# Expert stage of a two-block model: how each pair of experts gets its token rows, four more weight tiles, and the place of the overflow loop

## The chip, the cores and the metric

The kernel runs on one core of one Trainium2 chip. Its time is the device time in microseconds (us). Before the change it is 2866.49 us, the median of 3 runs (2866.16 to 2867.72). The engines are PE (TensorE, matmuls), DVE (VectorE), ACT (ScalarE), POOL (GpSimd) and SP (SyncE, which here only issues DMAs). The engines run side by side and meet at semaphores.

## The reference

Two transformer-like blocks run one after the other on 512 tokens of width 1024. The change touches only the last part of the second block, a mixture of experts (`hier_moe`), and the final norm behind it:

```python
ht = h.reshape(T, D)                                   # T = 512 tokens, D = 1024
grp = jnp.argmax(g_logits, axis=-1)                    # one of 4 groups
top_p, top_i = lax.top_k(e_prob, TOP_K)                # 2 of the group's 8 experts
expert = grp[:, None] * EXP_PER_GROUP + top_i          # 2 of 32 experts per token
...
xb = ht[tok]                                           # rows of the tokens of one expert
hid = jax.nn.silu(xb @ w_gate[e]) * (xb @ w_up[e])     # 1024 -> 512
return hid @ w_down[e]                                 # 512 -> 1024
...
y = jnp.zeros((T, D), f32).at[buf_tok].add(y_blocks * buf_w[:, None])
x = x + y ; return rmsnorm(x, final_norm_g)
```

Each expert has three float32 matrices of 2 MiB, so 32 experts read 192 MiB.

## The kernel before, in words

**Pairs of experts.** The stage `Moe.run` works on 16 pairs. Each expert has 64 slots for tokens, so a pair fills 128 slots: the first expert is in rows 0 to 63 and the second in rows 64 to 127. `route` works out for each of a token's two choices its slot, 64 * expert + rank. Tokens beyond an expert's 64 slots are done by `overflow`, a loop whose count `nov` is read at run time (`For_i`, L1860). With these inputs the loop's body doesn't run: no matmul of its shapes is in the trace.

**Gathering tokens by matmul.** `rows` turns the 8 tiles of the residual into token rows and splits each into a high and a low half (`h2`, in 16 tiles `x` of the pool `px`). `gather` (L1726) builds 0/1 matrices by comparing slot numbers with a row 0, 1, 2, ... (`iota`): `A` in bf16, one for each choice, and `oh`, their sum. Every second pair, 64 matmuls (L1748) multiply `h2` by `oh` and give the tokens of two pairs, 256 columns, which ACT scales into `X`. `gs` multiplies `A` by three bf16 pieces of the gate weight and of the norm's factor.

**The work of a pair.** `up` multiplies by the gate matrices (32 matmuls on the trace, L1772), then by the up matrices (32 more, L1772). `down` transposes the result (4, L1815), lets `turned` transpose `oh` (4, L1801) into `oT`, and multiplies by the down matrices (32, L1824). `combine` (16 matmuls, L1842, and 8 additions on DVE, L1850) adds the result of the pair before into the tokens; it is woven into the next pair by `add`, so that no engine waits for it.

**Weights.** `load_w` issues 12 DMAs of 1 MiB for a pair from SP, in the order gate, up, down. They go into 13 tiles `we`, which exist while the stage before still runs, and 4 tiles `we2`: 17 in turn. A load waits until the tile that it overwrites has been read by its last matmul, and all loads wait in one queue in order.

**Order.** PE's order in the pairs is as written (`manual_schedule`); a scheduler places the other engines' instructions. Pairs 0 to 13 run first, then their last `combine`, then the loop `overflow`, then pairs 14 and 15. At the loop all engines meet, and SP goes into it only when its loads have landed; `load(14, AH)` therefore puts few loads of the next pair ahead of it.

Of the kernel before, what the change touches and what calls it, by code (L numbers as in the profile page):

```python
# [115 lines left out]
class Ker:  # L116
    def __init__(self, ctx, tc, I):
        self.tc, self.nc, self.I = tc, tc.nc, I
        self.scopes = []
        self.base = ctx.enter_context(tc.tile_pool(name="base", bufs=1))  # L120
        self.px = ctx.enter_context(tc.tile_pool(name="px", bufs=16))
# [7 lines left out]
        nc.sync.dma_start(self.ident, I["c_ident"])  # L129

# [1328 lines left out]
def consts3():  # L1459
# [4 lines left out]
    c["c_iota"] = np.ascontiguousarray(np.broadcast_to(np.arange(256, dtype=f), (128, 256)))  # L1464
# [19 lines left out]
SBM = dict(we2=4, X=1, oh=4, A=8, hid=1, hT=1, y=4, oT=1, rel=2, gs=2)  # L1484
AH = 3
# [3 lines left out]
class Moe:  # L1489
    CAP = 64  # L1490

    def __init__(self, K, V):
# [7 lines left out]
        self.iota = cst("iota", (128, 256), I["c_iota"])  # L1500
# [62 lines left out]
    def load_piece(self, e):  # L1563

        def get(q, i, k, d=0):
            w, n = self.weights()[i]
            t = self.K.px.tile([128, 512], F32, name="rstd", tag="rstd", bufs=1)
# [5 lines left out]
    def rows(self, x3):  # L1573

        K, nc = self.K, self.nc
        self.h2 = [[None] * 2 for _ in range(4)]
        b = K.t("X", (128, 4, 512))
        at = [K.t("hid"), K.t("oT"), K.t("hT")] + [b[:, j, :] for j in range(4)]
        for h in range(2):
            for t in range(4):  # L1580
# [3 lines left out]
                hi, lo = K.xt(), K.xt()  # L1584
                if not at:
                    K.split(ps, hi, lo)
                else:
                    x = at.pop()
                    nc.scalar.copy(hi, ps)
                    nc.scalar.copy(x, ps)  # L1590
                    nc.gpsimd.tensor_sub(lo, x, hi.bitcast(F32))
                self.h2[t][h] = (hi, lo)
# [26 lines left out]
    def route(self):  # L1619
# [60 lines left out]
        self.gr = one("grs", (128, 3, 2, 4, 2), BF16)  # L1680
# [4 lines left out]
        for i in range(3):  # L1685
            nc.vector.tensor_copy(self.gr[:, i], gr)
            if i < 2:
                nc.vector.tensor_sub(gr, gr, self.gr[:, i])
# [37 lines left out]
    def gather(self, rel, n, follow=lambda X, k: None):  # L1726
# [3 lines left out]
        oh, A = [], []  # L1730
        for t in range(4):
            A.append([K.t("A", (128, n), BF16) for _ in range(2)])
            nc.vector.tensor_scalar(A[t][1], self.iota[:, 0:n], rel[:, 1, t:t + 1], None, op0=ALU.is_equal)  # L1733
            o = K.t("oh", (128, n), F32R)
            nc.vector.scalar_tensor_tensor(o, self.iota[:, 0:n], rel[:, 0, t:t + 1], A[t][1], op0=ALU.is_equal,  # L1735
                                           op1=ALU.add)
            oh.append(o)
        for t in range(4):
            nc.gpsimd.tensor_scalar(A[t][0], self.iota[:, 0:n], rel[:, 0, t:t + 1], None, op0=ALU.is_equal)
        X = K.t("X", (128, 8, n))  # L1740
        w = 512 // n
        for k0 in range(0, 8, w):
            ps = K.p("x", (128, w, n))
            for k in range(k0, k0 + w):
                c = slice((k % 4) * 128, (k % 4 + 1) * 128)
                for t in range(4):
                    for j in range(2):
                        nc.tensor.matmul(ps[:, k - k0, :], self.h2[t][k // 4][j][:, c], oh[t], start=(t == 0 and j == 0),  # L1748
                                         stop=(t == 3 and j == 1))
            for k in range(k0, k0 + w):  # L1750
                nc.scalar.activation(X[:, k, :], ps[:, k - k0, :], AF.Copy, scale=self.g[:, k:k + 1])
            for k in range(max(k0 - w, 0), k0):
                follow(X, k)
        for k in range(8 - w, 8):
            follow(X, k)

        def gs(p):
            m = min(n, 128)
            ps = K.p("x", (128, 3, 2))
            for i in range(8):  # L1760
                t, a = divmod(i, 2)
                nc.tensor.matmul(ps[0:m], A[t][a][:, p * 128:p * 128 + m], self.gr[:, :, a, t, :], start=(i == 0), stop=(i == 7))
            s = K.t("gs", (128, 4))
            nc.vector.tensor_reduce(s[0:m, 0:2], ps[0:m].rearrange("p j c -> p c j"), axis=AX.X, op=ALU.add)
            nc.vector.tensor_scalar(s[0:m, 2:3], s[0:m, 1:2], 0.5, None, op0=ALU.mult)
            nc.vector.tensor_mul(s[0:m, 3:4], s[0:m, 1:2], s[0:m, 2:3])
            return s
        return X, oh, gs
# [5 lines left out]
    def up(self, X, w, n_ex, gs, pg=None, then=lambda hid: None, between=lambda: None):  # L1774
# [4 lines left out]
        if pg is None:  # L1779
            pg = K.p("g")  # L1780
            for k in range(8):
                self.proj(pg, X, w, n_ex, 0, k)
        gs = gs()
        hid = K.t("hid")
        nc.scalar.activation(hid[n], pg[n], AF.Tanh, scale=gs[n, 2:3])
# [6 lines left out]
        nc.vector.scalar_tensor_tensor(hid[n], hid[n], gs[n, 3:4], pu[n], op0=ALU.mult, op1=ALU.mult)  # L1792
        return hid, gs

    def turned(self, n_ex, oh):

        K, nc = self.K, self.nc
        np_ = 64 * n_ex
        ps = K.p("y")
        for t in range(4):  # L1800
            nc.tensor.transpose(ps[0:np_, t * 128:(t + 1) * 128], oh[t].bitcast(F32), K.ident)  # L1801
        o = K.t("oT", dt=F32R)
        if np_ < 128:
            nc.gpsimd.memset(o[np_:128].bitcast(F32), 0.0)
        nc.vector.tensor_copy(o[0:np_], ps[0:np_])
        return o

    def down(self, w, n_ex, hid, gs, between):
# [9 lines left out]
        o = between()  # L1818
# [13 lines left out]
        return o, ys  # L1832

    def combine(self, o, ys, ts=range(4), first=False, done=None):

        K, nc = self.K, self.nc
        for t in ts:
            s = slice(t * 128, (t + 1) * 128)
            for d in range(2):
# [3 lines left out]
                if first:  # L1843
                    hi, lo = self.h2[t][d]
                    a = self.acc[t][d] = K.t("h")
                    nc.vector.tensor_add(a, ps, hi.bitcast(F32))
                    nc.vector.tensor_add(a, a, lo.bitcast(F32))
                else:
                    a = self.acc[t][d]
                    nc.vector.tensor_add(a, a, ps)  # L1850
# [3 lines left out]
    def overflow(self):  # L1854
# [5 lines left out]
        with tc.For_i(0, n, 1) as i:  # L1860
# [4 lines left out]
            X, oh, gs = self.gather(rel, 64)  # L1865
            w = self.load_piece(e)
            hid, g = self.up(X, w, 1, lambda: gs(0))
            self.combine(*self.down(w, 1, hid, g, lambda: self.turned(1, oh)))

    def run(self, ctx, x3, out):  # L1870
        K, nc, I = self.K, self.nc, self.K.I
        K.scope(ctx, "mo", SBM, PSM)
        self.acc = [[None] * 2 for _ in range(4)]
# [3 lines left out]
        next(steps)  # L1877
# [29 lines left out]
        def add(*ts):  # L1907
            if late:
                o, ys, first = late
                self.combine(o, ys, ts, first)  # L1910

        def pair(i):
            nonlocal X, oh, gs, late
            q, p = divmod(i, 2)
            load(i)
            pg = None
            if i == 0:
                pg = K.p("g")
# [90 lines left out]
```

## Time and profile before

| | |
|---|---|
| time of the profiled execution | 2866.79 us |
| its span | 2865.0 us |
| median of the runs shown | 2866.49 us |
| PE busy | 2787.5 us, 97% of the span |
| DVE, ACT, POOL busy | 1721.1 us, 1070.5 us, 179.0 us |
| mean TensorE clock granted | 0.986 |
| read from HBM | 415.91 MB |

All times below are us from the span's start, unless they are ns. The expert stage begins at about 2334 (the token rows) and ends with the span. PE is nearly always busy in every stage, so the share alone doesn't tell what a change is worth; what counts in the expert stage is how closely PE and the weight loads follow one another. [...]

### The profile page before, as it was taken

What the parts mean: (1) busy time and instruction counts of PE and PEld (TensorE: products, weight loads), DVE (VectorE), ACT (ScalarE), POOL (GpSimd) and SP (SyncE); (2) the same over time, 40 slices, a digit from 0 to 9 for tenths busy, and PEclk for the clock granted to TensorE, in tenths of its full rate; (3) what the DMA queues carried; (4) which work ended last, traced back from release to release, by engine and by line L of the source; (5) the groups of instructions that cost most, each with busy time, mean ns of one, the idle gap of its engine ahead of it and who ended that gap; (6) DMA issues with size and microseconds to landing.
All of it is one profiled execution on the core that took longest, in us unless ns stands there. A gap on an engine that the chain in (4) does not pass through costs nothing. (4 is left out here: it accounts for less than half of the span.)

```text
span 2865.0 us, 41006 instructions
## 1 busy us (share of the span) xinstructions
PE 2787.5 (97%) x15978; PEld 2027.6 (71%) x15978; DVE 1721.1 (60%) x3122; ACT 1070.5 (37%) x1992; POOL 179.0 (6%) x221
## 2 busy tenths in 40 slices
PE   8989999999999999998999999999999889999998
PEld 6779878888889888886776777777778664444543
DVE  6666666645566666648777778678775343333333
ACT  4355443333244433345544455445444231111112
POOL 3100000000000000013000000000013120000000
PEclk8999999999999999999999999999999989999999
DMA  5324222223234122234422233223238719999966
GB/s 171 96 67 146 75 82 95 96 96 105 95 112 146 59 96 95 94 114 142 139 75 84 87 90 103 82 78 98 65 110 322 269 64 400 417 415 420 419 269 265
DMA packets 176005, 447.70 MB, mean 156 GB/s; under 512 B 80928, under 2 KB 82144, under 8 KB 151232
## 3 DMA queue, kind: packets, MB, share of 16 engines
q1 hardware_dynamic: 175504, 444.16, 43.6%
q8 instruction: 127, 2.08, 0.3%
q0 software_dynamic: 304, 0.89, 0.1%
q14 instruction: 70, 0.57, 0.1%
HBM read 415.91 MB, written 29.08 MB: 155 GB/s over the span
## 5 line engine op out<-in xcount | busy, mean ns | idle before, releaser
L171 ACT CAST w<-wr 128x512 fp32r<-128x512 f32 x662 | 407.3, 620 | 758.5 <-PE ps_d L217 659.2
L216 PE MATMUL ps_d<-x,w 128*128 128x512 f32 x1624 | 659.8, 406 | 0.7 <-ACT w L171 0.7
L218 PE MATMUL ps_d<-x,w 128*128 128x512 f32 x1624 | 653.8, 403 | 4.1 <-DVE w L172 4.1
L217 PE MATMUL ps_d<-x,w 128*128 128x512 f32 x1624 | 654.3, 403 | 0.0
L172 DVE TENSOR_TENSOR w<-wr,w 128x512 fp32r<-128x512 f32 x662 | 471.3, 715 | 266.3 <-ACT w L171 261.6
L218 PEld LDWEIGHTS ps_d<-x,w 128*128 128x128 f32 x1624 | 306.1, 188 | 76.8 <-DVE w L172 4.7
L216 PEld LDWEIGHTS ps_d<-x,w 128*128 128x128 f32 x1624 | 306.5, 189 | 74.1 <-issue 4.3
L217 PEld LDWEIGHTS ps_d<-x,w 128*128 128x128 f32 x1624 | 306.6, 189 | 69.9 <-issue 2.9
L1772 PE MATMUL ps_g<-we,X 128*64 128x512 f32 x1024 | 226.8, 595 | 0.0
L216 PE MATMUL ps_d<-s,w 128*128 128x512 f32 x512 | 202.8, 396 | 0.0
L217 PE MATMUL ps_d<-s,w 128*128 128x512 f32 x512 | 202.6, 396 | 0.0
L218 PE MATMUL ps_d<-s,w 128*128 128x512 f32 x512 | 202.6, 396 | 0.0
L1772 PEld LDWEIGHTS ps_g<-we,X 128*64 128x64 f32 x1024 | 71.1, 137 | 137.8 <-issue 136.5
L1824 PE MATMUL ps_y<-we,hT 128*64 128x512 f32 x512 | 113.6, 595 | 0.5 <-ACT hT L1817 0.5
L217 PEld LDWEIGHTS ps_d<-s,w 128*128 128x128 f32 x512 | 96.1, 188 | 23.4 <-DVE s L172 0.6
L216 PEld LDWEIGHTS ps_d<-s,w 128*128 128x128 f32 x512 | 96.1, 188 | 22.8
L218 PEld LDWEIGHTS ps_d<-s,w 128*128 128x128 f32 x512 | 96.1, 188 | 22.7
L216 PE MATMUL ps_a<-x,w 128*128 128x512 f32 x232 | 92.1, 405 | 8.4 <-DVE gt L1428 5.2
L217 PE MATMUL ps_a<-x,w 128*128 128x512 f32 x232 | 93.3, 403 | 0.1
L218 PE MATMUL ps_a<-x,w 128*128 128x512 f32 x232 | 92.2, 399 | 0.0
L1824 PEld LDWEIGHTS ps_y<-we,hT 128*64 128x64 f32 x512 | 35.1, 137 | 67.7 <-issue 64.4
L1850 DVE TENSOR_TENSOR h<-h,ps_x 128x512 f32<-128x512 f32 x120 | 76.7, 681 | 7.4 <-PE ps_x L1842 6.4
(574 smaller groups left out, 4146.9 us busy)
## 6 DMA issues: line engine op xcount, KB each, us to landing
we<-in_w_exp_gate SPq DMA_DIRECT2D x64, 1024.0 KB, 12.0
we<-in_w_exp_up SPq DMA_DIRECT2D x64, 1024.0 KB, 12.1
we<-in_w_exp_down SPq DMA_DIRECT2D x64, 1024.0 KB, 12.6
wr<-in_w_in SPq DMA_DIRECT2D x83, 512.0 KB, 3.6
wr<-in_ffn_w_up SPq DMA_DIRECT2D x64, 512.0 KB, 3.2
wr<-in_ffn_w_down SPq DMA_DIRECT2D x32, 512.0 KB, 3.2
wr<-in_w_in_c SPq DMA_DIRECT2D x24, 512.0 KB, 3.2
wr<-in_w_in_ab SPq DMA_DIRECT2D x16, 512.0 KB, 4.2
```

The lines of the kernel that those rows point to most:

```text
L171: nc.scalar.copy(hi, x)
L172: nc.vector.tensor_sub(lo, x, hi.bitcast(F32))
L216: nc.tensor.matmul(ps, whi, xhi, start=start, stop=False)
L217: nc.tensor.matmul(ps, whi, xlo, start=False, stop=False)
L218: nc.tensor.matmul(ps, wlo, xhi, start=False, stop=stop)
L1772: self.nc.tensor.matmul(ps[e * 64:e * 64 + 64, :], X[:, k, e * 64:e * 64 + 64], w(e, i, k), start=(k == 0), stop=(k == 7))
L1824: nc.tensor.matmul(py[e * 64:e * 64 + 64, :], hT[:, f, e * 64:e * 64 + 64], w(e, 2, f, d), start=(f == 0), stop=(f == 3))
L1850: nc.vector.tensor_add(a, a, ps)
```

## The change

- `rows` copies the token rows whole (no split) into the accumulators `acc` and writes them to a DRAM buffer `hr` (8 DMAs of 256 KB, on SP). `combine` thereby loses its special first case.
- `index` replaces the 0/1 matrix `oh`. For one pair at a time it builds `A` with 128 columns (4 comparisons on POOL, 4 on DVE), multiplies it by token numbers (`tok`, 8 small matmuls), and turns the sum into a row number. Then come the 8 small matmuls by `gr`, as before.
- `gather` is now one indirect DMA on POOL's queue: 128 rows of 4 KB out of `hr` into `G` (512 KB). `columns` transposes `G` (8 transposes) and scales into `X` (2 multiplications on DVE).
- This runs a pair ahead (`ahead`): the comparisons of pair i+1 are placed at the start of pair i, the small matmuls between its gate and up matmuls, the transposes before its down matmuls.
- `back` gets `oT` by one comparison on DVE; the transposes of `turned` go.
- `we2` grows from 4 to 8 tiles (21 in all). The pool `px` (17 tiles of 2 KB) is placed on the other side of the memory and ends with the stage before.
- The loop `overflow` stands behind pair 0, with 8 of pair 2's loads ahead of it.

```diff
-SBM = dict(we2=4, X=1, oh=4, A=8, hid=1, hT=1, y=4, oT=1, rel=2, gs=2)
-AH = 3
+SBM = dict(we2=8, X=1, G=1, Xo=1, Go=1, A=8, hid=1, hT=1, y=4, oT=1, rel=2, gs=3, ix=2)
...
     def rows(self, x3):
...
-                self.h2[t][h] = (hi, lo)
+                a = self.acc[t][h] = K.t("h")
+                nc.scalar.copy(a, ps)
+                nc.sync.dma_start(self.hr[t * 128:(t + 1) * 128, h * 512:(h + 1) * 512], a)
...
-    def gather(self, rel, n, follow=lambda X, k: None):
+    def index(self, rel, n=128):
...
         for t in range(4):
...
+            A.append([K.t("A", (128, 128), BF16)[:, 0:n] for _ in range(2)])
+            for a, eng in enumerate((nc.gpsimd, nc.vector)):
+                eng.tensor_scalar(A[t][a], self.iota[:, 0:n], rel[:, a, t:t + 1], None, op0=ALU.is_equal)
+        yield
+        s, ix = K.t("gs", (128, 5)), K.t("ix", (128, 2))
+        def product(shape, of):
+            ps = K.p("x", shape)
             for i in range(8):
                 t, a = divmod(i, 2)
...
+                nc.tensor.matmul(ps[0:n], A[t][a], of(a, t), start=(i == 0), stop=(i == 7))
+            return ps[0:n]
+        nc.vector.tensor_reduce(s[0:n, 2:3], product((128, 2), lambda a, t: self.tok[:, t]), axis=AX.X, op=ALU.add)
+        nc.vector.tensor_scalar(ix[0:n, 0:1], s[0:n, 2:3], -1.0, 0.0, op0=ALU.add, op1=ALU.max)
+        self.token = ix.bitcast(I32)[:, 1:2]
+        nc.vector.tensor_copy(self.token[0:n], ix[0:n, 0:1])
+        yield
+        ps = product((128, 3, 2), lambda a, t: self.gr[:, a, t])
...
+    def gather(self, n=128, tag="G"):
+
+        G = self.K.t(tag, (128, 1024))
+        self.nc.gpsimd.indirect_dma_start(out=G[0:n], out_offset=None, in_=self.hr[:],
+                                          in_offset=bass.IndirectOffsetOnAxis(ap=self.token[0:n], axis=0))
+        return G
+
+    def columns(self, G, n=128, tag="X"):
...
+            for k in range(4):
+                nc.tensor.transpose(ps[:, k, :], G[0:n, (k0 + k) * 128:(k0 + k + 1) * 128], K.ident[0:n, 0:n])
+            nc.vector.tensor_mul(X[:, k0:k0 + 4, :], ps, self.g[:, k0:k0 + 4, None].to_broadcast([128, 4, n]))
+        return X
...
+    def back(self, n, s):
...
+        nc.vector.tensor_scalar(o[0:n], self.iota[0:n], 1.0, s[0:n, 2:3], op0=ALU.add, op1=ALU.is_equal)
...
+        def ahead(i):
...
+            part = self.index(rel)
+            next(part)
+            yield
+            next(part)
+            G = self.gather()
+            yield
+            yield next(part), G
...
+            def mid():
+                nonlocal coming
+                if i < 15:
+                    next(nxt)
+                    coming = next(nxt)
+                add(0)
+            hid = self.up(X, w, 2, gs, then, mid)
...
             def rest():
                 add(2, 3)
-                return self.turned(2, [x[:, s] for x in oh])
-            late = *self.down(w, 2, hid, g, rest), i == 0
...
+                if i < 15:
+                    columns.append(self.columns(coming[1]))
+            ys = self.down(w, 2, hid, gs, rest)
+            late = self.back(128, gs), ys
...
         with K.tc.manual_schedule(engines=PE):
-            for i in range(14):
-                pair(i)
+            load(0)
+            load(1)
+            pair(0)
             add(0, 1, 2, 3)
         late = None
-        load(14, AH)
+        load(2, 8)
         self.overflow()
         with K.tc.manual_schedule(engines=PE):
-            for i in (14, 15):
+            for i in range(1, 16):
                 pair(i)
-            self.combine(*late[:2], done=finish)
-
+            self.combine(*late, done=finish)
```

PE, one pair in the middle of the stage, before. `y`, `oT` belong to the combine of the pair before, `hid` is transposed for the down matmuls, `oh` and `x` are the 0/1 matrix and the split token rows.

```order
L1842 MATMUL ps_x<-y,oT 128x512 x4
L1772 MATMUL ps_g<-we,X 64x512 x16
L1842 MATMUL ps_x<-y,oT 128x512 x4
L1815 MATMUL ps_y<-ident,hid 128x128 x4
L1842 MATMUL ps_x<-y,oT 128x512 x8
L1801 MATMUL ps_y<-ident,oh 128x128 x4
L1824 MATMUL ps_y<-we,hT 64x512 x16
L1748 MATMUL ps_x<-oh,x 128x256 x64
```

PE at the same place, now. The row by `grs` is the last of the 8 small matmuls, behind the 8 by `tokb`.

```order
L1745 MATMUL ps_x<-grs,A 128x6
L1842 MATMUL ps_x<-y,oT 128x512 x4
L1787 MATMUL ps_g<-we,X 64x512 x16
L1842 MATMUL ps_x<-y,oT 128x512 x4
L1815 MATMUL ps_y<-ident,hid 128x128 x4
L1842 MATMUL ps_x<-y,oT 128x512 x8
L1772 MATMUL ps_x<-ident,G 128x128 x8
L1824 MATMUL ps_y<-we,hT 64x512 x16
L1787 MATMUL ps_g<-we,X 64x512 x16
```

The 64 matmuls of every second pair are gone and the 4 transposes of `oh` have become 8 of `G`, which wait for the indirect DMA.

SP from the last weight loads before the stage to the loop, now (before, the loads of the first 14 pairs stand there without a break).

```order
L1568 DMA we_21363<-in_w_exp_gate 128x2048
L1595 DMA hr<-h 128x512 x8
L1568 DMA we_21365<-in_w_exp_gate 128x2048
L1568 DMA we_21367<-in_w_exp_up 128x2048
...
L1568 DMA we<-in_w_exp_down 128x2048 x3
L1568 DMA we<-in_w_exp_gate 128x2048 x4
L1568 DMA we<-in_w_exp_up 128x2048 x4
L1853 TENSOR_LOAD nov
```

The 8 writes of token rows stand ahead of the last 6 of the 21 first loads; 11 more loads stand ahead of the loop's count, all others behind it.

POOL from the head of the stage to the pairs behind the loop, now (before, it has there 24 comparisons for `A` in a row).

```order
L1738 TENSOR_SCALAR A<-iota,rel 128x128 x8
L1761 DMA G<-hr,ix 128x1024 x2
L1853 TENSOR_LOAD nov
...
L1738 TENSOR_SCALAR A<-iota,rel 128x128 x6
L1761 DMA G<-hr,ix 128x1024
L1738 TENSOR_SCALAR A<-iota,rel 128x128 x4
```

The first gather stands behind the comparisons of pairs 0 and 1, and each later gather behind two comparisons of the pair after it.

## Rows read from the trace of the kernel before

**Rows 1.** The page: span in 40 slices, busy tenths of PE and DMA.
```profile
PE   8989999999999999998999999999999889999998
DMA  5324222223234122234422233223238719999966
```
**Rows 2.** Timeline of PE, pairs 2 and 3: start, us, engine, line, what.
```profile
2421.32 7.09 PE L1772 MATMUL ps_g<-we,X 128*64 128x512 f32 x32
2428.34 0.36 PE L1762 MATMUL ps_x<-grs,A 128*128 128x6 bf16 x8
...
2440.14 0.60 PE L1801 MATMUL ps_y<-ident,oh 128*128 128x128 f32 x4
2440.67 7.09 PE L1824 MATMUL ps_y<-we,hT 128*64 128x512 f32 x32
...
2447.58 7.04 PE L1772 MATMUL ps_g<-we,X 128*64 128x512 f32 x32
...
2473.89 7.84 PE L1748 MATMUL ps_x<-oh,x 128*128 128x256 f32 x64
2481.66 7.09 PE L1772 MATMUL ps_g<-we,X 128*64 128x512 f32 x32
```
**Rows 3.** Windows: stretch, us, five engines' busy us, PE clock, DMA share, GB/s.
```profile
2352.00:2358.00 6.00, 6.00 (x32) 5.29 (x34) 0.72 (x2) 1.68 (x4) 0.55 (x1) 0.65 0.01 3
2700.00:2750.00 50.00, 50.00 (x268) 24.79 (x266) 16.25 (x29) 7.72 (x15) 0.04 (x1) 1.00 1.01 417
2768.00:2783.00 15.00, 12.59 (x53) 5.10 (x51) 8.15 (x13) 1.38 (x2) 0.00 (x0) 1.00 0.00 1
2816.00:2820.00 4.00, 4.00 (x22) 1.43 (x20) 0.75 (x1) 0.69 (x1) 0.00 (x0) 1.00 1.02 424
2832.00:2836.00 4.00, 4.00 (x20) 1.15 (x16) 0.00 (x0) 0.00 (x0) 0.00 (x0) 1.00 0.05 20
```
**Rows 4.** Waits of SP's queue from 2100 on: us in total, times, longest.
```profile
SPq L1557 <- PE ps_g L1772: 199.8, 41, 31.6
SPq L1860 <- SPq L1860: 10.5, 2, 8.0
```
**Rows 5.** Timeline at the head of the stage.
```profile
2330.95 38.00 SPq L1557 DMA_DIRECT2D we<-in_w_exp_up  x4
2347.00 0.16 DVE L1664 TENSOR_TENSOR slot<-slot,y 128x8 f32<-128x8 f32 x1
2347.26 2.97 POOL L1739 TENSOR_SCALAR A<-iota,slot 128x256 bf16<-128x256 f32 x3 [0.20 <-DVE y L1688]
2369.72 7.09 PE L1772 MATMUL ps_g<-we,X 128*64 128x512 f32 x32
2385.93 4.46 PE L1772 MATMUL ps_g<-we,X 128*64 128x512 f32 x20
```
**Rows 6.** DMA issues from 0 to 60, last row 2300 to the end: us to landing.
```profile
rpb_s<-v POOLq DMA_DIRECT2D x1, 480.0 KB, 8.1
mask<-in_c_namask POOLq DMA_DIRECT2D x1, 256.0 KB, 6.2
v<-in_rpb POOLq DMA_DIRECT2D x1, 7.3 KB, 5.0
...
X<-in_g_fin SPq DMA_DIRECT2D x1, 512.0 KB, 3.7
```
**Rows 7.** Timeline around the overflow loop.
```profile
2775.55 0.73 PE L1842 MATMUL ps_x<-y,oT 128*128 128x512 f32 x2
2784.06 0.17 DVE L1923 TENSOR_SCALAR rel<-slot 128x8 f32<-128x8 f32 x1 [1.52 <-issue]
2787.38 9.88 PE L1748 MATMUL ps_x<-oh,x 128*128 128x256 f32 x60 [0.40 <-DVE oh L1735]
```
**Rows 8.** Timeline of PE, the last pair's down matmuls and the last combine.
```profile
2840.00 7.09 PE L1824 MATMUL ps_y<-we,hT 128*64 128x512 f32 x32
2847.02 1.36 PE L1842 MATMUL ps_x<-y,oT 128*128 128x512 f32 x3
```

More of the change, by code (lines that the diff above doesn't have):

```diff
@@ L1723, in route @@
         yield
-    def gather(self, rel, n, follow=lambda X, k: None):
+    def index(self, rel, n=128):
         K, nc = self.K, self.nc
-        oh, A = [], []
+        A = []
         for t in range(4):
[L1732 to L1759, printed above, removed]
@@ L1772, in proj, with up @@
             self.nc.tensor.matmul(ps[e * 64:e * 64 + 64, :], X[:, k, e * 64:e * 64 + 64], w(e, i, k), start=(k == 0), stop=(k == 7))
-    def up(self, X, w, n_ex, gs, pg=None, then=lambda hid: None, between=lambda: None):
+    def up(self, X, w, n_ex, gs, then=lambda hid: None, between=lambda: None):
         K, nc = self.K, self.nc
         n = slice(0, 64 * n_ex)
[L1779 to L1783, printed above, removed]
+        pg = K.p("g")
+        for k in range(8):
+            self.proj(pg, X, w, n_ex, 0, k)
         hid = K.t("hid")
-        nc.scalar.activation(hid[n], pg[n], AF.Tanh, scale=gs[n, 2:3])
+        nc.scalar.activation(hid[n], pg[n], AF.Tanh, scale=gs[n, 3:4])
         then(hid)
@@ L1791, in up @@
             self.proj(pu, X, w, n_ex, 1, k)
[L1792 to L1806, printed above, removed]
+        nc.vector.scalar_tensor_tensor(hid[n], hid[n], gs[n, 4:5], pu[n], op0=ALU.mult, op1=ALU.mult)
+        return hid
     def down(self, w, n_ex, hid, gs, between):
@@ L1817, in down @@
         nc.scalar.copy(hT[:, :, n], ps[:, :, n])
-        o = between()
+        between()
         ys = []
@@ L1831, in down, with combine @@
             ys.append((a, b))
-        return o, ys
-    def combine(self, o, ys, ts=range(4), first=False, done=None):
+        return ys
+    def combine(self, o, ys, ts=range(4), done=None):
         K, nc = self.K, self.nc
@@ L1842, in combine @@
                     nc.tensor.matmul(ps, o[:, s], ys[d][j], start=(j == 0), stop=(j == 1))
[L1843 to L1850, printed above, removed]
+                a = self.acc[t][d]
+                nc.vector.tensor_add(a, a, ps)
             if done:
@@ L1864, in overflow @@
             nc.vector.tensor_scalar(base, base, -64.0, None, op0=ALU.add)
-            X, oh, gs = self.gather(rel, 64)
+            steps = self.index(rel, 64)
+            next(steps)
+            next(steps)
+            X = self.columns(self.gather(64, "Go"), 64, "Xo")
+            gs = next(steps)
             w = self.load_piece(e)
-            hid, g = self.up(X, w, 1, lambda: gs(0))
-            self.combine(*self.down(w, 1, hid, g, lambda: self.turned(1, oh)))
+            hid = self.up(X, w, 1, gs)
+            self.combine(self.back(64, gs), self.down(w, 1, hid, gs, lambda: None))
     def run(self, ctx, x3, out):
@@ L1908, in add @@
             if late:
-                o, ys, first = late
-                self.combine(o, ys, ts, first)
-        def pair(i):
[L1913 to L1918, printed above, removed]
-                X, oh, gs = self.gather(self.slot, 256, lambda X, k: self.proj(pg, X[:, :, 0:128], ws[0][0], 2, 0, k))
-                next(steps)
-            elif p == 0:
-                rel = K.t("rel", (128, 2, 4))
-                nc.vector.tensor_scalar(rel, self.slot, float(-256 * q), None, op0=ALU.add)
-                X, oh, gs = self.gather(rel, 256)
-            s = slice(p * 128, (p + 1) * 128)
+                self.combine(*late, ts)
+        def ahead(i):
+            rel = K.t("rel", (128, 2, 4))
+            nc.vector.tensor_scalar(rel, self.slot, float(-128 * i), None, op0=ALU.add)
+            part = self.index(rel)
[5 more added lines that the diff above has]
+            yield next(part), G
+        def pair(i):
+            nonlocal late, coming
+            if i > 1:
+                load(i)
+            (gs, G), X = coming, columns.pop()
             w = ws[i][0]
+            if i < 15:
+                nxt = ahead(i + 1)
+                next(nxt)
             then = lambda hid: i == 15 and nc.scalar.activation(r[:, 0:1], hid[:, 0:1], AF.Sqrt, bias=K.eps, scale=0.0)
-            hid, g = self.up(X[:, :, s], w, 2, lambda: gs(p), pg, then, lambda: add(0))
+            def mid():
+                nonlocal coming
+                if i < 15:
+                    next(nxt)
+                    coming = next(nxt)
+                add(0)
+            hid = self.up(X, w, 2, gs, then, mid)
             add(1)
```

68 lines of the change are left out of this document (40 added, 28 removed).

## The prediction

> **What bounds the kernel now.** I read the page's slices first: PE is busy everywhere, and DMA is nearly full only in the last sixth, the expert stage [rows 1]. So this stage has two candidates, and I measured both over the same piece of work, two pairs.
>
> PE: the gate matmuls of pair 2 start at 2421.32 and those of pair 4 at 2481.66, so two pairs take 60.34 us without a gap [rows 2]. DMA: two pairs load 24 tiles of 1,048,576 bytes. Where the queue is surely full the 16 engines move 424 GB/s at a busy share of 1.02 [rows 3], so a tile takes 2.47 us and 24 take 59.4 us. In the middle DMA runs at 417 GB/s, also with a share of 1.01 [rows 3]. So PE sets the pace, by 1.0 us in two pairs and no more. SP's queue says the same: it waits for PE to release a gate or up tile, 41 times and 199.8 us [rows 4]. Whoever takes work from PE in the middle of this stage meets the DMA floor at once.
>
> At the end the two part. After the loop, for which DMA stood still from 2768 to 2783, the last weights have landed by about 2832, when the rate falls to 20 GB/s [rows 3]. PE ends its last down matmuls at 2847.0 [rows 8], 15 us behind. This is where PE's savings are worth something.
>
> **The change part by part.**
>
> *PE in a pair.* A pair without the 64 gather matmuls takes 2473.89 - 2447.58 = 26.3 us now; the 64 add 7.8 us to every second pair [rows 2]. They go. The 4 transposes of `oh` (0.53 us from 2440.14 to 2440.67) become 8 (+0.53 us), and 8 small matmuls come on top of 8 (+0.36 us, the price of the present 8) [rows 2]. A pair is then 27.2 us, 3.0 us less than the mean 30.2. Pair 1, with no combine in it, is 4.5 us shorter.
>
> *DMA in a pair.* A gather moves 524,288 bytes, 1.24 us at 424 GB/s. A pair then needs 12 x 2.47 + 1.24 = 30.9 us of DMA, against 27.2 us of PE. The order of the two is reversed. The four new tiles (21 for 17) only lengthen PE's lead: it is used up at 3.7 us a pair. From both sides: the gather can't take less than its bytes at 424 GB/s, because every engine is then full; a row of 4 KB may cost as much as one of 8 KB, which is 2.5 us a gather. I take 1.24, nearest to the rate shown.
>
> *The gather's wait.* From the end of the gate matmuls to the transposes there are 2440.14 - 2428.34 = 11.8 us now [rows 2], 12.2 with the second 8 matmuls. The row numbers need both groups of small matmuls (0.7 us) and a few short DVE steps, and on POOL the gather stands behind two comparisons of 128 columns that wait for the same matmuls. Three of 256 columns take 2.97 us [rows 5], so I take 0.5 us each (between 0 and 1.0). That leaves 10.5 us for the gather. What does it take? No row shows an indirect DMA. POOL's DMAs at the start, beside busy SP loads, land after 5.0 us (7.3 KB), 6.2 us (256 KB) and 8.1 us (480 KB) [rows 6]. Bounds: 5.0 and twice 6.2, 12.4; I take 8.1, the nearest in size. So it is hidden, save in pairs 0 and 1, where the 4.4 us of combine matmuls are missing and about 2 us show, in the lee of DMA.
>
> *The head.* The slots are ready at 2347.2 and POOL's comparisons follow [rows 5]: 4 of pair 0 (2.0 us), two groups of small matmuls (0.7), 4 of pair 1 which stand ahead of the gather (2.0), the gather (8.1), 4 transposes and a DVE multiplication (1.7), and with 0.3 us between, pair 0's gate starts at 2362. The row writes wait for ACT's copies, which end about when the slots are ready, so they have some 5 us to land before the gather. The gate's 7.0 us become about 9.5: after the loop, where PE had stood, 60 gather matmuls took 9.88 us, while 64 take 7.84 us in the middle [rows 2, 7], and the windows show a granted clock of 0.65 at the present head [rows 3]. So the up matmuls start at about 2372, for 2369.7 now. The rest of the pair is 2385.93 - 2369.72 = 16.2 us [rows 5], plus 0.9: pair 0 ends at 2389. The head loses 3 us.
>
> *The loop.* It follows pair 0 with the combine alone in front: 2784.06 - 2775.55 = 8.5 us as now [rows 7], so 2398 by PE and DVE. SP waits there for its own loads, as it does now (10.5 us in two waits) [rows 4]. The 11 loads ahead of the loop start when pair 0's first gate tiles are released (2368) and need 27 us, plus some waiting for the last releases, plus 2.4 us to land (an idle queue lands 512 KB in 3.7 us, of which 1.24 us is moving) [rows 6]: 2399. Pair 1 starts at 2400.5. At its old place the loop and a slow gather behind it go.
>
> *The sum.* By PE alone: 2400.5 + 22.7 + 14 x 27.2, less 1.4 us that pair 15 doesn't need = 2802.6 for the end of the last down matmuls. By DMA: pair 1's first tiles are released at 2404, then 192 - 33 = 159 tiles (13 + 8 + 11 were loaded by then, and the 33rd found its tile free at the loop) x 2.473 = 393.2 us and 14 gathers x 1.24 = 17.4 us, so 2814.6; 2.4 us to land, 2817.0; the last tile is used from the second quarter of the last down matmuls on, so three quarters follow, 5.3 us: 2822.3. DMA decides, 20 us behind what PE could do. Now it is 2847.0 [rows 8], so 24.7 us go. The tail behind it is as now. The profiled execution took 2866.79 us, 0.3 above the median: 2866.8 - 24.7 - 0.3 = 2842 us.
>
> **The rivals.**
>
> *Late gather, slower.* Place: the 8 transposes of `G` stand before the down matmuls, and PE can do nothing else while they wait. Price: every us above 10.5 costs 1 us in each of pairs 2 to 14, and in pairs 0 and 1 the price starts 4.4 us earlier. PE's end by itself is 2802.6, so it passes the DMA's 2822.3 at about 11.2 us, and passes today's 2847.0 at about 13 us. At 14 us it is 2802.6 + 2 x 7.9 + 13 x 3.5 = 2864, a time of 2883. For it: the weight loads keep the same 16 engines full (share 1.01) [rows 3]. Against it: the three POOL rows, which had busy engines too [rows 6].
>
> [...]
>
> *A dear gather on DMA.* If 128 scattered rows take 2.5 us of all engines, 14 x 1.24 = 17.4 us are added to the DMA sum: 2859 us. At three times it is 2877 us.
>
> *PE keeps the pace.* If weights came as fast as PE asked, the end would be 2802.6 and the time 2822 us. Against it: 424 GB/s at a share of 1.02 is the ceiling of every full window [rows 3].
>
> *The change doesn't do what it says:* more tiles and less PE work bring nothing since DMA was as good as full before. That holds in the middle, where a pair even gets 0.7 us longer than now (30.9 for 30.2), but not for the 15 us at the end and the 15 us stop at the loop. It would take a head 20 us later than worked out to reach no change.
>
> **How the numbers follow.** DMA decides as worked out: 0.62, own range 2832 to 2852 (head 10 us off either way, or the gather near 12 us). Late gather: 0.15, of which 0.04 under today's time and 0.11 above. Dear gather: 0.13, of which 0.07 ends clearly faster, 0.03 about the same, 0.03 slower. PE keeps the pace: 0.05. No gain from other causes: 0.05. A measurement of this kernel tells about 0.2% from no change, 5.7 us. Faster: 0.62 + 0.05 + 0.07 + 0.04 = 0.78; same: 0.03 + 0.05 = 0.08; slower: 0.11 + 0.03 = 0.14. The range goes from 2830 to 2862: up to twice the gather's bytes, and a gather at its upper bound of 12.4 us (PE's end 2802.6 + 2 x 6.3 + 13 x 1.9 = 2840, time 2859).
>
> **What would show it.** Right: DMA at about 424 GB/s from 2404 to 2815 without a gap; SP's waits for PE in the second half gone, and PE waiting for weights instead, some 3.7 us a pair, from about pair 10 on; pairs of 27 us first, 31 us then; the transposes of `G` without an idle time before them; pair 0's gate near 2362 and pair 1's near 2400. Wrong: idle time of PE before the transposes in every pair (late gather); a rate under 410 GB/s with the share at 1.0 (dear gather); pairs of 27 us to the end (PE keeps the pace); a gap of DMA of more than 10 us around the loop.

## The result, and the profile after

The kernel after takes 2835.86 us (2835.15 to 2836.80, four runs), the kernel before 2867.1 beside it: a ratio of 0.9885, with a 95% interval of 0.9868 to 0.9903. That is 31 us less. The forecast was 2842 us, so direction and range hold. But the sum behind it does not: of the 31 us the expert stage gives 11, where 24.7 were forecast, and some 20 come from the stages ahead of it, for which nothing was forecast. That the total came so close is luck.

The split is read at a landmark that both kernels have, the first routing product. First before, then after (start, us, engine, line):

```profile
2341.78 0.79 PE L1647 MATMUL ps_g<-y,su 128*128 128x128 f32 x2 [4.92 <-DVE y L1642]
```
```profile
2320.84 0.80 PE L1650 MATMUL ps_g<-y,su 128*128 128x128 f32 x2 [3.03 <-DVE y L1645]
```

The stage starts 20.9 us earlier in these two profiles. The amount varies between executions: in the seven profiles of kernels that have the same stages ahead as after (after and experiments 1, 4, 5, 6, 7 and 9) this product stands at 2318.8 to 2329.6, so 12 to 23 us earlier than in the one profile of before, 18 on average. From there to the end of the span it is 2865.0 - 2341.8 = 523.2 us before and 2833.4 - 2320.8 = 512.5 us after. Below, "stage time" always means this, and a time "behind routing" counts from this product.

**Where the 20.9 us come from.** The page's costliest groups (busy us, mean ns), the products of weights `w` with an operand half `x` and with an `s` tile. In the program both are of the type fp32r, which it uses for the high and low halves of split float32 numbers; the trace prints f32. Before:

```profile
L216 PE MATMUL ps_d<-x,w 128*128 128x512 f32 x1624 | 659.8, 406 | 0.7 <-ACT w L171 0.7
...
L216 PE MATMUL ps_d<-s,w 128*128 128x512 f32 x512 | 202.8, 396 | 0.0
```
After:
```profile
L219 PE MATMUL ps_d<-x,w 128*128 128x512 f32 x1624 | 653.4, 402 | 0.8 <-ACT w L174 0.8
...
L219 PE MATMUL ps_d<-s,w 128*128 128x512 f32 x512 | 202.7, 396 | 0.0
```

The products with `x` got cheaper, those with `s` did not, and the change touches no instruction of either. The three lines of `x` lose 6.4, 6.6 and 6.3 us, the same products in the merge (`ps_a`) 3.7 us together. The timeline shows it in one product: 24 of them in a row, at a granted clock of 1.00, a share of full speed, in both, before and then after.

```profile
519.66 0.40 PE L216 MATMUL ps_d<-x,w 128*128 128x512 f32 x1
...
525.26 0.40 PE L216 MATMUL ps_d<-x,w 128*128 128x512 f32 x1
```
```profile
519.71 0.39 PE L219 MATMUL ps_d<-x,w 128*128 128x512 f32 x1
...
525.15 0.39 PE L219 MATMUL ps_d<-x,w 128*128 128x512 f32 x1
```

Start to start 5.60 / 24 = 233.3 ns before, 5.44 / 24 = 226.7 ns after. What the change did to these products is to move the pool `px`, in which `x` lies, from the left of SBUF to the right.

**The stage.** PE and DMA in the page's 40 slices, which answer to [rows 1]:

```profile
PE   8989999999999999998999999999999877999997
DMA  5324223333234123334422333223238838999997
```

PE, one pair, answering to [rows 2]; and the gate of a late pair:

```profile
2414.09 7.04 PE L1787 MATMUL ps_g<-we,X 128*64 128x512 f32 x32
...
2433.08 1.25 PE L1772 MATMUL ps_x<-ident,G 128*128 128x128 f32 x8
...
2441.18 1.89 PE L1787 MATMUL ps_g<-we,X 128*64 128x512 f32 x8
...
2722.51 4.03 PE L1787 MATMUL ps_g<-we,X 128*64 128x512 f32 x17
2727.67 3.65 PE L1787 MATMUL ps_g<-we,X 128*64 128x512 f32 x14 [1.14 <-DMA we<-in_w_exp_gate]
```

A pair takes 2441.18 - 2414.09 = 27.1 us, and the transposes of `G` stand without idle time in front. Eight pairs in a row take that; from pair 11 on the gates start 31.1 us apart and PE waits for weights. SP's queue has turned as forecast (answers to [rows 4]): it waits for its own DMAs often and briefly, and for a gate or up tile of PE 55.6 us in all, for 199.8 before. The long ones of these, up to 19.2 us, lie at the head of the stage; behind 2420 no weight load waits for one.

```profile
SPq L1568 <- DMA we<-in_w_exp_gate: 93.7, 43, 3.5
SPq L1568 <- PE ps_g L1787: 55.6, 20, 19.2
```

Windows, answering to [rows 3]: around the loop, late in the stage, and where the last weights land (the last two figures are DMA's share and GB/s, the one before is PE's granted clock).

```profile
2380.00:2384.00 4.00, 0.50 (x2) 0.30 (x4) 0.72 (x3) 0.00 (x0) 0.45 (x1) 0.76 0.18 76
2384.00:2388.00 4.00, 4.00 (x12) 1.13 (x10) 1.15 (x6) 0.00 (x0) 2.10 (x4) 0.50 0.61 193
2388.00:2392.00 4.00, 4.00 (x20) 1.28 (x18) 0.00 (x0) 0.00 (x0) 0.00 (x0) 0.89 0.45 129
...
2700.00:2750.00 50.00, 47.86 (x233) 19.50 (x234) 20.76 (x48) 3.92 (x6) 6.90 (x10) 1.00 1.01 421
...
2806.00:2810.00 4.00, 3.98 (x16) 1.28 (x17) 2.44 (x5) 0.00 (x0) 0.00 (x0) 1.00 0.72 297
```

From 2392 on DMA is full but for 2412 to 2416 (a share of 0.78, 270 GB/s), late in the stage at 421 GB/s; in the 12 us before 2392 it moves a third of that. The head and the loop, answering to [rows 5, 7]:

```profile
2326.48 2.58 POOL L1738 TENSOR_SCALAR A<-iota,rel 128x128 bf16<-128x128 f32 x4 [48.97 <-DVE grs L1689]
2330.03 2.58 POOL L1738 TENSOR_SCALAR A<-iota,rel 128x128 bf16<-128x128 f32 x4 [0.96 <-PE ps_x L1745]
2332.78 1.21 POOL L1761 DMA_INDIRECT G<-hr,ix  x1 [0.17 <-issue]
2341.87 1.94 PE L1772 MATMUL ps_x<-ident,G 128*128 128x128 f32 x8 [11.83 <-DMA G<-hr,ix]
2343.74 9.15 PE L1787 MATMUL ps_g<-we,X 128*64 128x512 f32 x32
...
2383.28 0.17 DVE L1910 TENSOR_SCALAR rel<-slot 128x8 f32<-128x8 f32 x1 [4.63 <-SPq L1854]
2383.50 9.74 PE L1787 MATMUL ps_g<-we,X 128*64 128x512 f32 x32 [5.85 <-DVE rel L1910]
```

Pair 0's gate starts 22.9 us behind routing and pair 1's 62.7, both slow (9.15 and 9.74 us, for 7.04 in the middle; the granted clock is 0.50 until 2347 in the first and until 2388 in the second, after PE had stood for the gather and at the loop, and 1.00 from 2348 and from 2389 on). The transfers, with the time to land (answers to [rows 6]), and the end (answers to [rows 8]):

```profile
we<-in_w_exp_gate SPq DMA_DIRECT2D x58, 1024.0 KB, 21.1
G<-hr,ix POOLq DMA_INDIRECT x16, 9.0
```
```profile
2806.97 8.18 PE L1824 MATMUL ps_y<-we,hT 128*64 128x512 f32 x32
2815.08 1.35 PE L1842 MATMUL ps_x<-y,oT 128*128 128x512 f32 x3
```

### The profile page after: what moved, and what is told of

Its sections match the earlier page's. It is cut to its first block, busy times and chain, and to the rows that moved or that the text cites. A ratio compares the mean times of both kernels' runs of the same rounds, so it can differ in the third digit from the quotient of the medians.

```text
span 2833.4 us, 40564 instructions
## 1 busy us (share of the span) xinstructions
PE 2731.4 (96%) x15658; PEld 1978.3 (70%) x15658; DVE 1722.4 (61%) x3203; ACT 1039.7 (37%) x1921; POOL 194.7 (7%) x262
## 5 line engine op out<-in xcount | busy, mean ns | idle before, releaser
L1787 PE MATMUL ps_g<-we,X 128*64 128x512 f32 x1024 | 242.7, 605 | 14.1 <-DVE rel L1910 5.9
L1787 PEld LDWEIGHTS ps_g<-we,X 128*64 128x64 f32 x1024 | 77.4, 139 | 164.1 <-issue 139.5
L1824 PE MATMUL ps_y<-we,hT 128*64 128x512 f32 x512 | 121.5, 604 | 0.8 <-DMA we<-in_w_exp_down 0.4
## 6 DMA issues: line engine op xcount, KB each, us to landing
we<-in_w_exp_gate SPq DMA_DIRECT2D x64, 1024.0 KB, 20.8
```

The lines of the kernel that those rows point to most:

```text
L1787: self.nc.tensor.matmul(ps[e * 64:e * 64 + 64, :], X[:, k, e * 64:e * 64 + 64], w(e, i, k), start=(k == 0), stop=(k == 7))
L1824: nc.tensor.matmul(py[e * 64:e * 64 + 64, :], hT[:, f, e * 64:e * 64 + 64], w(e, 2, f, d), start=(f == 0), stop=(f == 3))
```

## The experiments

Ratios are to the kernel before, run on the same chip beside them.

**1. px alone on the right.** Is the pool's place the cause of the 21 us?

```diff
-        self.px = ctx.enter_context(tc.tile_pool(name="px", bufs=16))
+        self.px = ctx.enter_context(tc.tile_pool(name="px", bufs=16, side="right"))
```


> The kernel before with one edit: the pool of the operand halves (px) lies on the right of SBUF, and nothing else is changed. After the change the products L216 to L218 of the operand halves start 227.9 ns apart, before it 232.8 ns (4338 of them, with 656 more in the merge), and the stage begins 21 us earlier. Theory A, the place of px alone does that: 5000 products by 4.9 ns is 24 us less, so 2843 to 2848 us, and 227 to 228 ns between the products here as well. Rival B, the 21 us come from something else that the change does (the shorter program, the expert stage's own buffers): 2865 to 2869 us as before, and 232 to 233 ns.

2851.4 us, 0.9937 (0.9923 to 0.9950): 15 us less, 14 to 22 by the interval, with one argument changed. The timeline at the place shown above:

```profile
519.61 0.39 PE L218 MATMUL ps_d<-x,w 128*128 128x512 f32 x1
...
525.05 0.39 PE L218 MATMUL ps_d<-x,w 128*128 128x512 f32 x1
```

Again 24 products in 5.44 us, as in after, and its stage time is before's (522.9). Until the merge begins, some 210 us ahead of routing, it has gained 16.5 us, after 17.2. In the merge PE idles more in this profile (12.8 us from 2200 to 2316, for 10.4), with a granted clock of 0.83 from 2260 to 2270, where after has 1.00. The median lies 3 us above A's range; that the merge is the reason in every execution is not shown. The cause is A, not B.

**2. The weights moved by 896 bytes.** Is it the part of SBUF, or how the two operands of a product lie to each other?

```diff
+            gap = mid.enter_context(tc.tile_pool(name="gap", bufs=1, side="right"))
+            nc.vector.memset(gap.tile([128, 224], F32, name="gap"), 0.0)
             K.scope(mid, "W", dict(wr=3, w=14, yr=2, rs=1), side="right")
```


> The kernel before with px left where it was, and the pool of the split weights moved down by 896 bytes, so that a weight tile and an operand half begin at the same place within 2048 bytes (1120), as they do after the change (2016 and 2016). Theory A1, what counts is how the moving and the stationary operand of a product lie to each other within 2 KB: 227 to 228 ns between products and 2843 to 2848 us. Rival A2, what counts is in which part of SBUF the operands lie, low and high before, both high after: no change, 232 to 233 ns and 2865 to 2869 us.

2844.9 us, 0.9923 (0.9909 to 0.9936): A1. The timeline at the same place as above, with `px` still on the left:

```profile
519.81 0.39 PE L217 MATMUL ps_d<-x,w 128*128 128x512 f32 x1
...
525.25 0.39 PE L217 MATMUL ps_d<-x,w 128*128 128x512 f32 x1
```

5.44 / 24 = 226.7 ns. Most of the `s` tiles came to lie well too (their mean went from 233.4 to 229.5 ns), so this does more than moving `px` did.

**3. The probe.** Which distances are good?

```diff
+        for (i, mo, j, so) in combos:          # regions i, j; offsets mo, so in bytes
+            for n in range(24):
+                mv = R[i][:, mo // 4 + n % 3 * 512:][:, :512]
+                st = R[j][:, 2048 + so // 4 + n * 5 % 14 * 128:][:, :128]
+                nc.tensor.matmul(ps, st, mv, start=(n == 0), stop=(n == 23))
```


> TensorE alone, nothing of the reference is computed: groups of 24 fp32r products of 128x512, the moving and the stationary operand taken from thirteen regions of 16 KB (64 pairs of regions, both at the start of their slots), and then one pair of regions with the moving operand 0 to 2016 bytes and the stationary 0 to 480 bytes off. Theory A1 (place within 2 KB): all 64 pairs of regions alike, and among the 102 offsets groups at 227 and others at 232 to 238 ns a product. Theory A2 (part of SBUF): the 64 differ by region, the offsets don't. Theory A3 (the operands' place matters only where other engines read and write SBUF beside them): all 166 groups alike.

The timeline of the groups with the stationary operand at 0 and the moving one at 0, 32, 64 and 96, then at 224, 256, 384 and 512 bytes; a group's time is the next row's start less its own:

```profile
354.94 5.60 PE L45 MATMUL ps<-rm,rj 128*128 128x512 f32 x24
360.38 5.77 PE L43 MATMUL ps<-rm,rj 128*128 128x512 f32 x24
365.99 5.67 PE L45 MATMUL ps<-rm,rj 128*128 128x512 f32 x24
371.49 5.77 PE L43 MATMUL ps<-rm,rj 128*128 128x512 f32 x24
...
393.92 5.76 PE L43 MATMUL ps<-rm,rj 128*128 128x512 f32 x24
399.52 5.63 PE L45 MATMUL ps<-rm,rj 128*128 128x512 f32 x24
404.98 5.75 PE L43 MATMUL ps<-rm,rj 128*128 128x512 f32 x24
410.57 5.62 PE L45 MATMUL ps<-rm,rj 128*128 128x512 f32 x24
```

5.44 us at 0, 5.61 at 32, 5.50 at 64, 5.60 at 224, 5.46 again at 256, 5.59 at 384. With the first matmuls of each group left out, over all 102 groups, a product takes 226.6 to 227.8 ns where the two operands are a multiple of 256 bytes apart, 228.7 to 229.0 at 64 more (moving less stationary), and 232 to 234 at the other multiples of 32. One group of the nine at 64 doesn't fit: with the moving operand at 1120 and the stationary at 32 it takes 233.4, and why is not shown. With the stationary operand at 32, 64, 128, 256 or 480 bytes the numbers shift along: what counts is the distance modulo 256. All 64 pairs of regions, which were tried at distance 0 alone, are alike (226.7), save the group at the very start. So A1, in a sharper form, and neither A2 nor A3: no other engine worked beside these. By the addresses in the built programs, `x` begins at 96 and `w` at 224 modulo 256 before (distance 128); after, both begin at 224.

**4. The loop back at its late place.**

```diff
-            pair(0)
+            for i in range(14): pair(i)
             add(0, 1, 2, 3)
         late = None
-        load(2, 8)
+        load(14, 8)
         self.overflow()
```


> The kernel after with the overflow loop back behind pair 13 and eight tiles of pair 14 asked for ahead of it, the rest as it is. The trace of after shows DMA at 76, 193 and 129 GB/s for the 12 us around the loop behind pair 0 (some 8 us lost) and then 420 GB/s to the end. Theory: DMA sets the end, so a loop that has 20 us of transfers in flight beside it costs nothing and the gap behind pair 0 goes: 2826 to 2832 us, DMA at about 420 GB/s through the loop. Rival: the loop costs DMA at the late place as much as it did at the early one (all engines meet there, and no load is asked for meanwhile): 2834 to 2842 us, with a gap of 8 us or more near 2770.

2834.4 us, 0.9886 (0.9871 to 0.9901): the same as after. Its runs go from 2827.2 to 2835.8 us. The profiled one is the fastest of them, and there the stage takes 506.5 us, 6 less than in after, of which 2.4 us lie between routing and the first comparison of `A`, since the routing products ran at a granted clock of 1.00 in this execution, for 0.58 in after (experiment 9). Pair 1's gate starts 28.6 us after pair 0's in place of 39.8, but DMA has its gap at the late place.

```profile
2748.00:2752.00 4.00, 0.00 (x0) 0.00 (x0) 0.00 (x0) 0.00 (x0) 0.00 (x0) 0.50 0.82 334
2752.00:2756.00 4.00, 1.46 (x4) 0.53 (x6) 1.39 (x6) 0.00 (x0) 1.27 (x2) 0.50 0.12 51
```

Eight tiles didn't cover it: PE stood 9.3 us before pair 14's gate. Neither theory as put: the median lies in the rival's range, but the gap, some 4 us at these two shares, is half of what it said. By the time over all runs no difference between the places is shown.

**5. Seventeen tiles.** What are the four new tiles worth?

```diff
-SBM = dict(we2=8, ...
+SBM = dict(we2=4, ...
-        load(2, 8)
+        load(2, 4)
```


> The kernel after with four we2 tiles in place of eight, so 17 weight tiles as before, and four loads ahead of the loop in place of eight. Theory: DMA sets the end, and until pair 0 gives its first tiles back it can fill only what tiles there are; four tiles fewer are 4 x 2.47 us less done by then, so about 10 us more: 2844 to 2848 us, with the pairs at 31 us from pair 7 or 8 on in place of pair 10. Rival: the head's gap is filled anyway and the tiles only deepen the queue: under 2839 us.

2840.5 us, 0.9908 (0.9892 to 0.9925): 5 to 7 us worse than after where the theory had 10, though the pairs come to 31 us two sooner, as it said. The rest is in the head:

```profile
2335.65 1.21 POOL L1761 DMA_INDIRECT G<-hr,ix  x1 [0.17 <-issue]
...
2340.31 1.94 PE L1772 MATMUL ps_x<-ident,G 128*128 128x128 f32 x8 [7.40 <-DMA G<-hr,ix]
```

Here SP issues two weight loads in the 7 us before the first gather, and DMA is no longer full beside it (276 GB/s at a share of 0.7 from 2327 to 2340, where after has 389 at 1.01): the rows are there 3.5 us after GpSimd has issued it (2340.31 - 2336.86). In after SP issues six, DMA is full until the rows land (shares of 1.00 to 1.02 from 2328 to 2344), and that takes 7.9 us (2341.87 - 2333.99). Pair 0's gate starts 18.0 us behind routing for 22.9, and 12.9 us behind the first comparison of `A` for 17.1 to 17.6 in the profiles with eight tiles (experiment 9). So the head takes back 4 to 5 us of what four tiles give.

**6. No gathers after the first**, and **7. two thirds of the weights.** Does DMA set the end, and what does a gather cost it?

```diff
-            G = self.gather()
+            self.G0 = G = self.gather() if i == 0 else self.G0
```


> The kernel after with the gather issued for pair 0 alone; pairs 1 to 15 transpose pair 0's rows again (so the output is not the reference's). Comparisons, token products and transposes stay. Theory: a pair's DMA falls from 31.1 to 29.7 us (12 x 2.47), still over TensorE's 27.1, so 14 x 1.2 to 1.4 us goes: 2816 to 2820 us, and 29.7 us a pair in the last pairs. Rival, a dear gather: over 2 us each, the last pairs near 28 us or less and 2815 us. Rival, a gather that lies beside the weights for nothing: 31 us a pair still, and 2834 to 2838 us.


```diff
+                if i == 2 and es[0] >= 4:
+                    ws[key] = ws[q, 0, j] ...      # down reads the gate tile, nothing is loaded
+                    continue
```


> The kernel after, but from pair 2 on only the gate and up tiles are loaded and the down products read the gate tiles (so the output is not the reference's): 8 tiles a pair in place of 12, every instruction of TensorE kept. Theory: DMA decides from pair 10 on, TensorE is 18 us behind; without DMA's limit the pairs stay at 27.1 us to the end: last down near 2789 in place of 2807 and 2816 to 2820 us. Rival: something else (the gather's wait, the copy of h, the code) makes the last pairs 31 us: no change, 2834 to 2838 us.

Without gathers 2813.4 us (0.9820, 0.9804 to 0.9837), and the last pair takes 2760.75 - 2730.89 = 29.9 us from gate to gate; with fewer weights 2812.4 us (0.9815, 0.9799 to 0.9832), and 2762.68 - 2735.58 = 27.1 us. First 6, then 7:

```profile
2730.89 4.46 PE L1787 MATMUL ps_g<-we,X 128*64 128x512 f32 x18
...
2760.75 1.46 PE L1787 MATMUL ps_g<-we,X 128*64 128x512 f32 x6
```
```profile
2735.58 7.04 PE L1790 MATMUL ps_g<-we,X 128*64 128x512 f32 x32
...
2762.68 1.89 PE L1790 MATMUL ps_g<-we,X 128*64 128x512 f32 x8
```

The time without gathers alone would fit the dear gather as well (2815 us). But the stage is 24.4 us shorter in this profile, and 9.8 of them lie ahead of pair 2's gate; from there on it is 14.7 us for 13 gathers. And DMA is as full and moves as much without gathers as with them (experiment 6; 421 GB/s in after):

```profile
2700.00:2750.00 50.00, 49.10 (x242) 18.78 (x238) 15.36 (x38) 4.02 (x6) 2.35 (x4) 1.00 1.01 420
```

So a gather costs DMA 31.1 - 29.9 = 1.2 us, what its bytes take (524,288 at 421 GB/s, 1.25 us); it is neither dear nor free. And the end is DMA's: PE's last down matmuls start at 2781.3 when weights are no limit, 26 us ahead of after. Both came out 3 to 4 us under their ranges; in both profiles pair 2's gate was earlier than in after as well (83.5 and 86.2 us behind routing, for 93.2).

**8. Every operand in place.** If the rule holds, the `s` products have the same to give.

```diff
-            self.scope(ctx, "ff", dict(s=32, u=4, gp=3, cv=3))
+            self.scope(ctx, "ff", dict(s=32, u=4, gp=3, cv=3), pad=96)   # likewise 32, 192, 192, 96
```


> The kernel after with pads of 32, 192, 192, 96 and 96 bytes at the head of five pools of the earlier stages, so that every operand of the fp32r products there (s, q, kv, pt, S beside x) begins at the same place within 256 bytes as the weight tiles; nothing else is changed. In the probe a product took 226.7 ns where the two operands differ by a multiple of 256 bytes, 228.9 at 64 and 233 to 234 else. Theory: the 1515 products s by w go from 233.3 to 227 ns (9.5 us) and 760 half ones from 118 to 113.5 (3.4 us): 13 us less, 2820 to 2826 us. Rival: other engines (the split of the weights, the transfers) set the pace of these stages as soon as TensorE is faster: 2832 us or more.

2827.1 us, 0.9862 (0.9840 to 0.9883), 9 less than after, though the two intervals overlap. What it does to the products is plain: the `s` products, at a mean of 233.3 ns in after, are at 227.0:

```profile
618.63 0.39 PE L222 MATMUL ps_d<-s,w 128*128 128x512 f32 x1
...
624.07 0.39 PE L222 MATMUL ps_d<-s,w 128*128 128x512 f32 x1
```

About 5 us of the 13 are missing by the products of 256 columns (`q` with `w`): they took 120.0 ns at distance 0, for 118 before, where 113.5 had been expected. What 512 columns showed doesn't hold for them.

**9. The head without GpSimd's queue**, then **10** the two together (8 with other pads, so that `q` stays where it was), **11** with the late loop.

```diff
-            part = self.index(rel)
+            part = self.index(rel, first=nc.vector if i < 2 else None)   # all comparisons on DVE
```


> The kernel after with the comparisons of pairs 0 and 1 all on VectorE (0.24 us each there, 0.6 on GpSimd), so that GpSimd has nothing in front of the first gather. In the trace of after the first token index is ready at 2330.2 and the gather is issued only at 2332.8, behind four comparisons of pair 1; the token products before it wait 0.36 us for each comparison. Theory: the chain to pair 0's gate is part of what DMA waits for at the head, so it gets 3 us shorter and so does the kernel: 2831 to 2834 us, pair 0's gate 20 us behind the routing products in place of 22.9. Rival: the head is covered (DMA has tiles to fill until pair 0 releases): 2835 to 2837 us.

> The aligned kernel with that change of the head, and with the q pool left where after has it (the half products with q took 120.0 ns aligned, 118 before). Theory, the gains add: 2827 less 1.4 less 3, so 2821 to 2824 us. Rival: the two take the same time away once (a stage that begins earlier meets the same DMA end): 2826 to 2828 us.

> The same with the overflow loop behind pair 13 and eight tiles of pair 14 ahead of it. In the one trace with the late loop DMA lost 6 us there and 6 fewer at the head. Theory: what the loop costs is the same at both places as long as the tiles asked for cover 20 us of it: within 2 us of the run without it. Rival: the late loop is cheaper, since TensorE has 4 us a pair to spare there: 4 to 6 us less. Rival: dearer, as the last pairs have no time to make it up: 3 us more or worse.

Nine: 2834.4 us, 0.9878 (0.9856 to 0.9900); by time alone it is not told from after. In its profile the stage took 509.3 us, 3.2 less, and pair 0's gate starts 20.8 us behind routing in place of 22.9; the stages ahead, which it doesn't touch, took 8.7 us more in that execution. The gate's place alone doesn't show the theory, though: it stands at 20.3 to 20.6 us in the profiles of 4, 6 and 7, which have after's head. The first two routing products took 0.49 us there and 0.80 in after; over the routing products the granted clock was 1.00 in 4 and 7 and 0.58 in after. After, then experiment 7, whose first routing product is at 2324.24:

```profile
2320.00:2324.00 4.00, 3.15 (x15) 3.16 (x16) 2.83 (x16) 0.08 (x1) 0.00 (x0) 0.58 0.18 69
```
```profile
2324.00:2328.00 4.00, 2.80 (x24) 2.69 (x24) 3.44 (x22) 2.05 (x4) 0.55 (x1) 1.00 0.19 73
```

The first comparison of `A` starts 5.6 us behind routing in after and 3.2 in 7. Counted from this comparison, pair 0's gate starts after 17.1 to 17.6 us in the five profiles with GpSimd's comparisons (after, 4, 6, 7, 8) and after 15.1 to 16.0 in 9, 10 and 11. So the chain is some 1.7 us shorter, not 3.

Ten: 2821.2 us, 0.9846 (0.9824 to 0.9867). The median is that of the sum, but the interval reaches the rival's 2826 to 2828 us too. Eleven: 2822.1 us, 0.9839 (0.9821 to 0.9856), no different. So ten and eleven beat both kernels, after by some 14 us.

**12. The probe for other shapes.** The same loop, with 256 columns and with fp32.

> TensorE alone again, nothing of the reference computed: groups of 24 products with the moving operand 0 to 224 bytes and the stationary 0 and 64 bytes off, for fp32r products of 128x256, fp32r of 128x512, and fp32 of 128x512 as in the expert stage. If the rule is one of the distance between the two operands within 256 bytes, all three kinds follow it: for 512 columns 226.7 ns at distance 0 and 233 else. The half ones took 120.0 ns at 0 in the aligned kernel, 117 to 118.5 at 32 and 224: expected 120 at 0 and the least, 113, at 64. [...]

Products of 512 fp32r columns repeat the first probe's numbers. Half ones cost 113.4 ns at a distance of 192 (not of 64, as expected), 119.8 at 0, and 117.4 to 119.6 else. An fp32 product, two instructions of 429.2 ns in the trace, takes 858.4 ns at every offset: for the expert matmuls, which are fp32, the probe shows nothing to gain.

## Why the prediction was right and where it was wrong

*What was left out.* The sum took everything ahead of the stage as unchanged. The change moves `px`, and of the 31.6 us between the two spans 20.9 lie ahead of the stage (12 to 23 over the profiles with this place of `px`); moved alone, it gave 15 us (14 to 22, experiment 1), by the operands' distance (experiments 2 and 3). Nothing in the prediction priced it: it counted the instructions that are added, removed or moved, and these 5640 products are none of that. The total came out 6 us off by luck, because this gain and an error of 14 us in the stage stood against each other. With the stage's 10.7 us alone the time would be an estimated 2856 us (2867.1 - 10.7), outside the prediction's own range of 2832 to 2852 for the case that DMA decides.

*PE in a pair:* 27.2 us forecast, 27.1 measured. *DMA in a pair:* 30.9 and 31.1; the gather's price of 1.24 us holds (experiment 6), so the dear gather falls. *The order of the two reverses at pair 10:* it does. *The gather's wait:* 8.1 us to land, 9.0 measured (8.4 to 9.6), within the 10.5 us that there are, so no wait in the middle, and 1.7 and 2.2 us in pairs 0 and 1. The late gather falls with it. Its sum took a gather of 14 us, which no run shows: the longest of the 16 in after landed after 9.6 us. The first gather landed 3.5 us after the end of its issue where two loads were issued ahead of it, and 7.9 where there were six (experiment 5). GpSimd's part of a gather took 0.95 to 1.21 us in all 16.

*DMA decides, 20 us behind PE:* right in kind, 26 us by the last down matmuls (experiment 7). "PE keeps the pace" falls.

*The stage's sum* is the step that failed by size: 498.5 us forecast (2842.1 - 1.8 - 2341.8), 512.5 measured. The 14 us are in three places.
- Pair 1's gate: 58.7 us behind routing forecast, 62.7 measured. 2.7 us of the 4.0 are ahead of pair 0's gate. From the first comparison to it the prediction had 14.8 us (2347.2 to 2362), and 17.3 were measured: four comparisons take 2.6 us for 2.0, those of pair 0 in front of the token products and those of pair 1 in front of the gather, and the rows land after 9.0 us for 8.1. Experiment 9 takes some 1.7 us of this away.
- From there to the last landing: 416.5 us forecast, about 425 measured (2383.5 to 2809). "Pair 1's first tiles are released at 2404" put the release 3.5 us into a gate at full speed. The gate ran at a granted clock of 0.50 for most of its 9.74 us (until 2388, 1.00 from 2389 on), and DMA was full only 8.5 us into it (a share of 1.01 from 2392 to 2396). And DMA goes at 420 to 421 GB/s, not 424, which is 3 to 4 us in 411.
- Behind it about 1 us: the last down matmuls wait for weights (8.18 us for 7.09).

"A gap of DMA of more than 10 us around the loop" was the sign against the head's sum. DMA ran at 76 to 193 GB/s for 12 us there, at shares of 0.18, 0.61 and 0.45, so 7 us were lost: not past the sign, but close to it. That the stage would gain 24.7 us was wrong; it gained 10.7.

## What to carry to other kernels

When a diff moves a pool or changes a size ahead of others, price it as an edit of every instruction that reads from there, and first compare a landmark in the unchanged part of both traces before any gain is credited to the part that was meant. Take the landmark from several profiles: here it moved by 11 us between executions of the same stages. Place the moving and the stationary operand of fp32r products of 512 columns at the same offset modulo 256 bytes (226.7 ns for 232 to 234 here); a pad does it (32 to 192 bytes in experiment 8). Where DMA is the floor (here 421 GB/s at a share of 1.01 from pair 11 on), a chain that ends in "first tile released" counts like bytes (4.0 of the 14 us here): shorten what stands on a queue in front of it (some 1.7 us in experiment 9), and take the price of the first matmuls after a standstill from the trace: here the gates behind the first gather and behind the loop began at a granted clock of 0.50 and took 9.15 and 9.74 us, for 7.04 in the middle.

## What the runs showed of the hardware that was not expected

- An fp32r product of 128x512 takes 227 ns where its operands' starts differ by a multiple of 256 bytes (in 64 pairs of places in SBUF), 229 at 64 more in eight of nine groups, and 232 to 234 else. With 256 columns it takes 113.4 to 119.8 ns, least at 192. fp32: 858.4 ns at every offset. What causes it is not shown.
- A 512 KB gather beside a full queue of weight loads costs that queue 1.2 us and lands 9.0 us after its start (8.4 to 9.6), 7.9 us after the end of its issue in the first one; with two loads issued ahead of it in place of six that was 3.5 us (experiment 5).
